# A conv-mixer block on one core: a norm's sum in four groups, sixteen native weight tiles, and a last pair of columns in halves

## The chip, the cores and the metric

The kernel runs on one core of a Trainium2 chip. The metric is the device time of one execution in microseconds (us), lower is better. Times of the instructions come from one profiled execution of the kernel.

## The reference

One decoder block in fp32 for 256 positions of width 2048. A condition vector c gives six modulation vectors of 2048 through a weight of 2048 by 12288. The mixer is a gated causal depthwise convolution; a squared-ReLU MLP of width 8192 follows.

```python
cond = silu(c)
sh1, sc1, g1, sh2, sc2, g2 = split(cond @ mod_w + mod_b, 6)
h = rms_norm(x, norm1_g) * (1.0 + sc1) + sh1
a, gt = split(h @ w_in + b_in, 2)            # 2048 -> 2 x 2048
u = a * sigmoid(gt)
u = depthwise_causal_conv(u, dw_w, 31 taps) + dw_b
y = silu(layer_norm(u, ln_g, ln_b)) @ w_out + b_out
x = x + (1.0 + g1) * y
h = rms_norm(x, norm2_g) * (1.0 + sc2) + sh2
x = x + (1.0 + g2) * (square(relu(h @ mlp_w1)) @ mlp_w2)
```

## The kernel before

Activations lie transposed: 128 features on the partitions, 256 positions along the free axis, so the width of 2048 is KT = 16 tiles called k. Weights are loaded as 1 MB tiles of 128 by 2048 in fp32.

**Two ways to multiply in fp32.** A *native* matmul takes the fp32 tiles as they are. A *split* one uses fp32r operands: ACT casts the weight to `hi`, DVE or POOL subtracts it to get `lo`, the activation is split in the same way into the two halves of `hl`, and PE adds hi times hi, hi times lo and lo times hi.

**The first stage.** `mod_c` holds rows of the modulation weight in a layout in which one output column group of 128 is a tile; `mod_col` forms one group on DVE as a multiply with the broadcast condition `cond` and an accumulated sum (line 299). For each k the scale column (SC1, finished as `amp`) and the shift column (SH1, finished as `modc`) are needed before h of that k exists. The load order is, for each k: scale column, shift column, and the tile `first` of k, which holds the rows of `w_in` for that k and all sixteen output tiles of the first eight jobs. These eight jobs are *held*: their sums stay in eight PSUM tiles (`mm`, `acc`, `small`, `row`) while k runs on the outside.

The loop over k issues on DVE, in a fixed order (`in_order`): the scale column of k, the low half of the activation of k - 1 (`act_low`, line 504), half of the weight's low part (`first_lo`, line 470) where k - 1 is split, for an even k the scaling of two x tiles by the norm factor r1 (line 514), the shift column, and the other half. ACT then forms h (line 523) and its high half (line 526), and PE multiplies. Ten of the sixteen k are in `NATIVE` and are multiplied natively (line 486); the other six are split (lines 463, 470 and 490 to 492).

**The first norm.** ACT squares x in eight pairs of tiles, PE adds over the partitions with a 128 by 128 matrix of ones (line 319), DVE scales the sum (line 336), ACT and DVE form the inverse root (lines 326 to 332) with one correction step. `rms_factor` is used again for the second norm.

**What follows.** ACT evacuates each held tile through a sigmoid and DVE multiplies (`gate`, lines 684 and 686). Jobs 8 to 15 are the remaining output pairs of `w_in`, each with two weight tiles (8,0), (8,1) and so on, split by ACT (line 200) and POOL (line 201), and multiplied in two halves of eight k each (lines 223 and 224). Between these matmuls lie steps of the modulation rows (line 241). Seven channel tiles are convolved on PE in a form that needs sixteen shifted copies of u on ACT each (`copy_wide`, line 646), one more with copies on both engines, the other eight on DVE tap by tap (lines 555 to 564). Then come layer norm, the output projection and the MLP, all with split weights.

**Order.** The order of instructions on each engine is settled when the program is built, by a scheduler that works with a simulated timeline, `issue_after` constraints and priorities (`urgent`). Loads are issued by SP in the order of one list; five `raw` buffers and four `first` buffers limit how far they run ahead. At run time each engine works its queue in order.

Of the kernel before, what the change touches and what calls it, by code (L numbers as in the profile page):

```python
# [14 lines left out]
P = 128  # L15
# [21 lines left out]
NATIVE = (1, 3, 5, 6, 8, 9, 11, 12, 14, 15)  # L37
# [20 lines left out]
SIDE = 14  # L58
POOLED = [("out", 0), ("out", 1), ("up", 0, 1), ("up", 0, 2)]
# [5 lines left out]
def conv_block(ctx: ExitStack, tc: tile.TileContext, x, vec, dwq, c_row, mod_r, mod_c, w_first, w_in, w_out, w1, w2, out):  # L65
# [48 lines left out]
    nc.scalar.activation(cz[:, :, 3], col("c", 0, KT), AF.Silu)  # L114
    modc = const.tile([P, 6 * KT], F32, name="modc")
# [3 lines left out]
    warm = const.tile([P, 1], F32, name="warm")  # L119

    def table(func, after):
        nc.scalar.activation(warm, after, func)
# [3 lines left out]

    raw = {}
# [3 lines left out]
    state = {"used": 0}  # L131
# [27 lines left out]
    def top_up():  # L159
        while todo and waiting[home(todo[0])] < room[home(todo[0])]:  # L160
# [13 lines left out]
            with tc.issue_after(state["load"].ins) if "load" in state else ExitStack():  # L174
                if key == ("first", KT - 1):
                    nc.sync.dma_start(raw[key][:, 0:HELD], source(key)[:, 0:HELD])
                    with tc.issue_after(state["load"].ins):
                        state["load"] = nc.sync.dma_start(raw[key][:, HELD:], source(key)[:, HELD:])
                else:
                    state["load"] = nc.sync.dma_start(raw[key], source(key))  # L180
# [7 lines left out]

    HALF = KT // 2
# [103 lines left out]

    def mod_col(at):
# [28 lines left out]
    def inverse_root(ms, src, scale, r, then=None):  # L323
# [114 lines left out]
    root_end = state["root_end"]  # L438
# [11 lines left out]
    first_parts = {}  # L450

    def first_hi(k):
        w = take(("first", k))
        if k in NATIVE:
            first_parts[k] = w
            return
        first_parts[k] = []
        for h in range(2):
# [489 lines left out]
```

## Time and profile before

| | us |
|---|---|
| Median of 3 runs | 1124.42 |
| Lowest and highest | 1123.18 and 1128.15 |
| The profiled execution's own time | 1122.33 |
| Its span, first to last instruction | 1120.5 |
| PE busy in the span | 1098.4 |
| DVE busy | 768.0 |
| ACT busy | 582.0 |
| POOL busy | 166.6 |

In a row of a timeline the first number is the start from the span's beginning, the second the duration, then engine, line, operation, output and inputs by the program's names, the shape, the count, and in brackets the idle time before it with what ended it. In a row of the windows the columns are the stretch, its length, the busy time of PE, of PE's weight loads, of DVE, ACT and POOL with instruction counts, the granted PE clock (1.00 is full), the mean share of the DMA engines and GB/s. A wait row gives the waiting instruction, what it waited for, the total, the count and the longest. A group row gives the instructions of one line with count, busy time, mean in ns, and the idle time before them.

### The profile page before, as it was taken

Reading aid. Unit: us, or ns where it says so; the run is one execution under the profiler, and the core shown is the slowest. Engines: PE = TensorE matmul, PEld = TensorE weight load, DVE = VectorE, ACT = ScalarE, POOL = GpSimd, SP = SyncE. Lnnn points to the kernel's source line nnn. Section 1 sums busy time; section 2 is a strip of 40 time slices with the busy share of each in tenths; the row PEclk is TensorE's granted clock in tenths of the full one; section 3 lists DMA queues with packets and bytes.
Section 4 is the critical chain, followed back from the end, with each engine's and each line's share of the span. In section 5 each row is a group of like instructions: output and inputs, shape, how many; then the busy total and the mean of one; then the engine's idle time right before and its main releaser. Section 6 shows DMA issues by size and latency. Waiting matters only on the chain.

```text
span 1120.5 us, 17425 instructions
## 1 busy us (share of the span) xinstructions
PE 1098.4 (98%) x7088; PEld 946.6 (84%) x7088; DVE 768.0 (69%) x1025; ACT 582.0 (52%) x806; POOL 166.6 (15%) x103
## 2 busy tenths in 40 slices
PE   6999999999999999999999999999999999999998
PEld 4888776766699998888888888888888888888888
DVE  3988689987489989887765555555555665555653
ACT  5222395664675587554445554444655444555441
POOL 0000086467533262000000000000000000000000
PEclk8999999999999999999999999999999999999999
DMA  9999979888599977888775555555554655555640
GB/s 384 420 421 420 418 307 346 349 322 318 207 390 350 371 283 276 290 350 299 273 259 192 190 193 194 193 191 193 189 190 165 211 188 188 188 188 188 209 139 29
DMA packets 41553, 293.35 MB, mean 262 GB/s; under 512 B 4609, under 2 KB 5121, under 8 KB 6401
## 3 DMA queue, kind: packets, MB, share of 16 engines
q1 hardware_dynamic: 41328, 292.17, 70.4%
q8 instruction: 55, 0.90, 0.3%
q14 instruction: 24, 0.20, 0.0%
q10 hardware_dynamic: 146, 0.08, 0.0%
HBM read 290.14 MB, written 2.10 MB: 261 GB/s over the span
## 4 chain that ended last, share of the span: by engine, by line
PE 86%; DMA 6%; DVE 6%; ACT 1%; issue 0%; POOL 0%; DVEq 0%; ACTq 0%; POOLq 0%
PE mm L223 45%; PE mm L224 24%; DMA raw<-mod_c 4%; PE mm L220 3%; DVE raw L299 3%; PE mm L219 3%; PE mm L221 3%; PE row L241 2%; PE mm L669 2%; DMA raw<-w_in 1%; PE small L319 1%; DVE lo L470 1%; PE mm L111 1%; PE mm L486 1%; PE acc L669 0%
## 5 line engine op out<-in xcount | busy, mean ns | idle before, releaser
L200 ACT ACTIVATE hi<-raw 128x1024 fp32r<-128x1024 f32 x320 | 335.3, 1057 | 355.9 <-PE mm L223 327.1
L201 DVE TENSOR_TENSOR lo<-raw,hi 128x1024 fp32r<-128x1024 f32 x272 | 333.6, 1232 | 234.4 <-ACT hi L200 233.4
L223 PE MATMUL mm<-hl,hi 128*128 128x512 f32 x1184 | 414.3, 393 | 0.4 <-DVE u L686 0.4
L223 PE MATMUL mm<-u,hi 128*128 128x512 f32 x1056 | 366.8, 390 | 0.0
L224 PE MATMUL mm<-hl,lo 128*128 128x256 f32 x1184 | 332.2, 281 | 0.0
L224 PE MATMUL mm<-u,lo 128*128 128x256 f32 x1056 | 297.7, 282 | 0.0
L223 PEld LDWEIGHTS mm<-hl,hi 128*128 128x128 f32 x1184 | 221.6, 187 | 58.2 <-issue 8.4
L223 PEld LDWEIGHTS mm<-u,hi 128*128 128x128 f32 x1056 | 198.2, 188 | 41.7 <-DVE small L332 0.2
L224 PEld LDWEIGHTS mm<-hl,lo 128*128 128x128 f32 x1184 | 223.7, 189 | 5.1 <-issue 4.2
L224 PEld LDWEIGHTS mm<-u,lo 128*128 128x128 f32 x1056 | 199.6, 189 | 0.1
L299 DVE SCALAR_TENSOR_TENSOR raw<-raw,cond 128x2048 f32<-128x2048 f32 x64 | 148.3, 2320 | 20.3 <-DMA raw<-mod_c 14.7
L201 POOL TENSOR_TENSOR lo<-raw,hi 128x1024 fp32r<-128x1024 f32 x48 | 118.1, 2482 | 198.0 <-ACT hi L200 198.0
L561 DVE SCALAR_TENSOR_TENSOR acc<-u,v,acc 128x256 f32<-128x256 f32 x224 | 94.7, 490 | 1.9
L220 PE MATMUL mm<-hl,hi 128*128 128x256 f32 x288 | 81.5, 284 | 0.8 <-DVE hl L209 0.8
L219 PE MATMUL mm<-hl,hi 128*128 128x256 f32 x288 | 80.5, 284 | 1.2 <-ACT hl L208 0.8
L221 PE MATMUL mm<-hl,lo 128*128 128x256 f32 x288 | 81.1, 283 | 0.0
L219 PEld LDWEIGHTS mm<-hl,hi 128*128 128x128 f32 x288 | 54.6, 192 | 2.8 <-ACT hl L208 1.7
L220 PEld LDWEIGHTS mm<-hl,hi 128*128 128x128 f32 x288 | 55.2, 192 | 1.6 <-DVE hl L209 1.2
L221 PEld LDWEIGHTS mm<-hl,lo 128*128 128x128 f32 x288 | 55.2, 192 | 0.0
L646 ACT ACTIVATE wide<-u 32x284 f32<-32x284 f32 x110 | 48.2, 438 | 2.7 <-DVE u L686 1.4
L423 ACT ACTIVATE two<-mm 128x512 f32<-128x512 f32 x70 | 40.9, 584 | 13.5 <-PE mm L224 13.5
L523 ACT ACTIVATE two<-two,modc,amp 128x256 f32<-128x256 f32 x16 | 9.6, 599 | 71.2 <-DVE modc L279 71.2
(166 smaller groups left out, 916.7 us busy)
## 6 DMA issues: line engine op xcount, KB each, us to landing
raw<-w SPq DMA_DIRECT2D x128, 1024.0 KB, 4.9
raw<-mod_c SPq DMA_DIRECT2D x64, 1024.0 KB, 10.8
raw<-mod_r SPq DMA_DIRECT2D x32, 1024.0 KB, 7.9
raw<-w_in SPq DMA_DIRECT2D x16, 1024.0 KB, 7.2
raw<-w_out SPq DMA_DIRECT2D x16, 1024.0 KB, 7.4
first<-w_first SPq DMA_DIRECT2D x15, 1024.0 KB, 16.1
x<-x SPq DMA_DIRECT2D x2, 1024.0 KB, 6.9
x<-x SPq DMA_DIRECT2D x1, 2048.0 KB, 9.8
```

The lines of the kernel that those rows point to most:

```text
L200: nc.scalar.activation(hi, w[:, ks, :], AF.Copy)
L201: end = engine.tensor_tensor(lo, w[:, ks, :], hi.bitcast(F32), op=ALU.subtract)
L219: nc.tensor.matmul(out_p, w, m[:, 0:T], start=begin, stop=False)
L220: nc.tensor.matmul(out_p, w, m[:, T : 2 * T], start=False, stop=False)
L221: state["mm_end"] = nc.tensor.matmul(out_p, lo[:, k % HALF, :], m[:, 0:T], start=False, stop=end)
L223: nc.tensor.matmul(p[:, c, :], hi[:, k % HALF, :], m, start=(k == 0), stop=(k == KT - 1))
L224: state["mm_end"] = nc.tensor.matmul(p[:, c, T : 2 * T], lo[:, k % HALF, :], m[:, 0:T], start=False, stop=(k == KT - 1), skip_group_check= ...
L241: state["row_end"] = nc.tensor.matmul(row_ps[0][32 * k : 32 * k + 32, :], cz[:, 4 * kg + k, 3 - b : 35 - b], w[:, 4 * k : 4 * k + 4, :], s ...
L299: nc.vector.scalar_tensor_tensor(w, w, 1.0, cb, op0=ALU.mult, op1=ALU.mult, accum_out=acc)
L423: nc.scalar.activation(t1, p[:, cs, T : 2 * T], AF.Copy)
L561: nc.vector.scalar_tensor_tensor(out, s, w, acc, op0=ALU.mult, op1=ALU.add)
L646: nc.scalar.activation(dst, src, AF.Copy)
```

## The change

Four things change. The first norm squares four pairs on ACT and four on DVE, and PE adds them with 32 columns of ones into four groups of 32 partitions, issued ahead of the first columns; one copy and one full matmul with the ones then add the groups up, each sum being there 32 times. The scaling of the sum is folded into the constants of the inverse root, in all three norms. All sixteen k are native, so the casts and subtractions of `first` tiles are gone. The two columns of the last k and its `first` tile are loaded in halves, and each of the two columns is formed by two half operations and one that adds the two sums. A table load for the inverse root is issued ahead.

```diff
-NATIVE = (1, 3, 5, 6, 8, 9, 11, 12, 14, 15)
+SPLIT_LOADS = [("col", SC1 * KT + KT - 1), ("col", SH1 * KT + KT - 1), ("first", KT - 1)]
...
+    table(AF.Abs_reciprocal_sqrt, cond[:, KT - 1, 0:1])
...
-                if key == ("first", KT - 1):
-                    nc.sync.dma_start(raw[key][:, 0:HELD], source(key)[:, 0:HELD])
-                    with tc.issue_after(state["load"].ins):
-                        state["load"] = nc.sync.dma_start(raw[key][:, HELD:], source(key)[:, HELD:])
+                if key in SPLIT_LOADS:
+                    first_half = nc.sync.dma_start(raw[key][:, 0:HALF], source(key)[:, 0:HALF])
+                    with tc.issue_after(first_half.ins):
+                        state["load"] = nc.sync.dma_start(raw[key][:, HALF:], source(key)[:, HALF:])
...
+    def mod_col_halves(at):
+        w = take(("col", at))
+        which, k = divmod(at, KT)
+        accs = [modc[:, at : at + 1], other]
+        for h in range(2):
+            ks = slice(h * HALF, (h + 1) * HALF)
+            in_order(lambda: nc.vector.scalar_tensor_tensor(
+                w[:, ks, :], w[:, ks, :], 1.0, cond[:, ks, :], op0=ALU.mult, op1=ALU.mult, accum_out=accs[h]
+            ))
+        in_order(lambda: nc.vector.scalar_tensor_tensor(
+            accs[0], accs[0], other, col("modb", at), op0=ALU.add, op1=ALU.add
+        ))
+        if which in amps:
+            in_order(lambda: nc.vector.tensor_tensor(amps[which][:, k : k + 1], accs[0], col("n1g", k), op=ALU.mult))
...
-        state["root_end"] = nc.scalar.activation(guess, guess, AF.Copy, scale=-0.5).ins
+        nc.scalar.activation(guess, guess, AF.Copy, scale=-0.5 * scale)
...
-        nc.vector.scalar_tensor_tensor(ms, ms, EPS, q, op0=ALU.add, op1=ALU.mult)
-        nc.vector.scalar_tensor_tensor(r, ms, 3.0, guess, op0=ALU.subtract, op1=ALU.mult)
+        nc.vector.scalar_tensor_tensor(ms, src, EPS / scale, q, op0=ALU.add, op1=ALU.mult)
+        nc.vector.scalar_tensor_tensor(r, ms, 3.0 / scale, guess, op0=ALU.subtract, op1=ALU.mult)
...
-    def rms_factor(total, ms, r):
-        nc.vector.tensor_scalar(ms, total, 1.0 / D, None, op0=ALU.mult)
-        return inverse_root(ms, total, 1.0 / D, r)
+    def rms_factor(total, ms, r, times=1):
+        return inverse_root(ms, total, 1.0 / (times * D), r)
...
-    mods(by_col(0))
     p = ps.tile([P, 512], F32, name="small", bufs=1)
     for k2 in range(HALF):
         s = two()
-        nc.scalar.activation(s, pair_of(xs, k2), AF.Square)
-        column_sum(p[:, 0:T], [s[:, j, :] for j in range(2)], k2 == 0, k2 == HALF - 1)
-    r1 = tmp.tile([P, T], F32, name="r", bufs=1)
-    rms_factor(p[:, 0:T], p[:, T : 2 * T], r1)
+        if k2 < HALF // 2:
+            nc.scalar.activation(s, pair_of(xs, k2), AF.Square)
+        else:
+            nc.vector.tensor_tensor(s, pair_of(xs, k2), pair_of(xs, k2), op=ALU.mult)
+        for j in range(2):
+            g = (2 * k2 + j) % 4
+            nc.tensor.matmul(p[32 * g : 32 * g + 32, 0:T], ones[:, 0:32], s[:, j, :], start=k2 < 2, stop=k2 >= HALF - 2)
+    mods(by_col(0))
+    with urgent():
+        part = two()[:, 0, :]
+        nc.scalar.activation(part, p[:, 0:T], AF.Copy)
+        p = ps.tile([P, 512], F32, name="row", bufs=1)
+        nc.tensor.matmul(p[:, 0:T], ones, part, start=True, stop=True)
+        r1 = tmp.tile([P, T], F32, name="r", bufs=1)
+        rms_factor(p[:, 0:T], p[:, T : 2 * T], r1, 32)
...
     def first_mm(k, h):
+        w = take(("first", k))
         with tc.issue_after(state["step_end"].ins) if k else ExitStack():
...
+                    step = nc.tensor.matmul(
+                        held[n][:, c, :], w[:, 2 * n + c, :], h, start=k == 0 and c == 0, stop=k == KT - 1, skip_group_check=True
+                    )
...
-            first_lo(k - 1, 0)
...
-            first_lo(k - 1, 1)
-            if k - 1 not in NATIVE:
-                first_mm(k - 1, None)
...
-        first_hi(k)
-        if k in NATIVE:
-            first_mm(k, h)
+        first_mm(k, h)
```

With the change the scheduler also writes other orders for the work behind the held tiles. ACT's queue from the first held tile on, in the kernel before and in the changed one (tiles in w_in's jobs named by job and half):

```
before:  gate 0; hi of 8,0 (2); gates 1, 2; hi of 8,1 (2); gates 3 to 7; wide x10; hi of 9,0 (2);
         wide x7; hi of 9,1 (1); wide x2; hi of 9,1 (1); wide x12; evacuation of job 8; ...
changed: gates 0 to 4; hi of 8,0 (2); gates 5 to 7; wide x11; hi of 8,1 (2); wide x7; hi of 9,0 (2);
         wide x3; hi of 9,1 (2); wide x11; evacuation of job 8; ...
```

On POOL the nine memsets' place moves from behind the third low half of job 8 to behind the first: they wait for the end of the held tiles. From job 10 on up to the output projection the order on ACT and POOL is nearly the same; around the first jobs of the MLP a few casts and modulations change places on ACT and DVE.

More of the change, by code (lines that the diff above doesn't have):

```diff
@@ L114, in conv_block @@
     nc.scalar.activation(cz[:, :, 3], col("c", 0, KT), AF.Silu)
+    state = {"used": 0}
     modc = const.tile([P, 6 * KT], F32, name="modc")
@@ L118, in conv_block @@
     amps = {w: const.tile([P, KT], F32, name=f"amp{w}") for w in (SC1, SC2)}
-    warm = const.tile([P, 1], F32, name="warm")
+    warm = const.tile([P, 2], F32, name="warm")
+    other = warm[:, 1:2]
     def table(func, after):
-        nc.scalar.activation(warm, after, func)
+        nc.scalar.activation(warm[:, 0:1], after, func)
+    table(AF.Abs_reciprocal_sqrt, cond[:, KT - 1, 0:1])
     def urgent():
         return tc.high_priority(offset=URGENT)
+    HALF = KT // 2
     raw = {}
@@ L448, in conv_block @@
     held += [pair(ps.tile([P, 512], F32, name=name, bufs=1)) for name in ("small", "row")]
-    first_parts = {}
-    def first_hi(k):
-        w = take(("first", k))
-        if k in NATIVE:
[L455 to L458, printed above, removed]
-            js = slice(h * HELD, (h + 1) * HELD)
-            hi = wts.tile([P, HALF, P], F32R, name="hi", bufs=6)
-            lo = wts.tile([P, HALF, P], F32R, name="lo", bufs=6)
-            with tc.issue_after(root_end):
-                nc.scalar.activation(hi, w[:, js, :], AF.Copy)
-            first_parts[k].append((hi, lo, w[:, js, :]))
-    def first_lo(k, h):
-        if k in NATIVE:
-            return
-        hi, lo, w = first_parts[k][h]
-        in_order(lambda: nc.vector.tensor_tensor(lo, w, hi.bitcast(F32), op=ALU.subtract))
     def in_order(op):
```

23 lines of the change are left out of this document (4 added, 19 removed).

## The prediction

> **What bounds the kernel now.** I read the page first, then the windows table by stage, then the waits of PE, then the timelines of each engine around the end of the first projection (k = 0 to 15 into eight held tiles).
>
> ```profile
> PE 1098.4 (98%) x7088; PEld 946.6 (84%) x7088; DVE 768.0 (69%) x1025; ACT 582.0 (52%) x806; POOL 166.6 (15%) x103
> 20.00:30.00 10.00, 4.39 (x25) 4.39 (x26) 7.51 (x9) 5.39 (x8) 0.00 (x0) 0.66 1.02 423
> 40.00:60.00 20.00, 19.25 (x131) 17.95 (x130) 19.82 (x24) 5.06 (x8) 0.00 (x0) 1.00 1.01 420
> 120.00:140.00 20.00, 18.34 (x103) 16.38 (x102) 11.80 (x17) 6.21 (x11) 2.68 (x2) 1.00 1.02 417
> PE mm L490 <- ACT hl L526: 6.1, 1, 6.1
> PE acc L492 <- DVE lo L470: 5.1, 6, 1.5
> PE mm L219 <- ACT hl L208: 0.8, 1, 0.8
> ...
> PE mm L223 <- DVE u L686: 0.4, 1, 0.4
> ```
>
> PE is 98% busy, yet up to 140 us the last three columns (clock, DMA share, GB/s) show the DMA engines full at 417 to 423 GB/s: there the stream sets the pace. The first two wait rows are PE's idle time in that stage. The last two are the first and last of the five waits that remain after 141 us, 2.8 us together. So from 141 us the end is PE's work, and the change is worth what it does to the time at which PE leaves the first projection, less any new wait behind it.
>
> **The first projection.** Where does the stream leave it?
>
> ```profile
> 94.24 2.29 DVE L299 SCALAR_TENSOR_TENSOR raw<-raw,cond 128x2048 f32<-128x2048 f32 x1 [1.56 <-DMA raw<-mod_c]
> 109.18 2.29 DVE L299 SCALAR_TENSOR_TENSOR raw<-raw,cond 128x2048 f32<-128x2048 f32 x1 [1.57 <-DMA raw<-mod_c]
> 116.75 2.29 DVE L299 SCALAR_TENSOR_TENSOR raw<-raw,cond 128x2048 f32<-128x2048 f32 x1 [2.27 <-DMA raw<-mod_c]
> 119.09 0.22 DVE L301 SCALAR_TENSOR_TENSOR amp<-modc,v 128x1 f32<-128x1 f32 x1
> 119.22 0.42 DVE L504 TENSOR_TENSOR hl<-two,hl 128x256 fp32r<-128x256 f32 x1
> 119.56 1.22 DVE L470 TENSOR_TENSOR lo<-first,hi 128x1024 fp32r<-128x1024 f32 x1
> 120.69 0.69 DVE L514 TENSOR_TENSOR two<-x,r 128x512 f32<-128x512 f32 x1
> 121.29 2.29 DVE L299 SCALAR_TENSOR_TENSOR raw<-raw,cond 128x2048 f32<-128x2048 f32 x1
> 123.62 0.16 DVE L279 TENSOR_TENSOR modc<-modc,v 128x1 f32<-128x1 f32 x1
> 123.88 0.60 ACT L523 ACTIVATE two<-two,modc,amp 128x256 f32<-128x256 f32 x1 [6.57 <-DVE modc L279]
> 126.99 3.62 PE L486 MATMUL mm<-two,first 128*128 128x256 f32 x16
> 133.90 3.62 PE L486 MATMUL mm<-two,first 128*128 128x256 f32 x16
> 139.94 1.03 PE L486 MATMUL row<-two,first 128*128 128x256 f32 x4
> L463 ACT ACTIVATE hi<-first 128x1024 fp32r<-128x1024 f32 x12 | 12.0, 1045 | 7.9 <-DMA first<-w_first 7.9
> L470 DVE TENSOR_TENSOR lo<-first,hi 128x1024 fp32r<-128x1024 f32 x12 | 14.6, 1219 | 0.0
> 25.61 0.80 PE L490 MATMUL mm<-hl,hi 128*128 128x256 f32 x2 [6.10 <-ACT hl L526]
> 29.14 0.28 PE L491 MATMUL mm<-hl,hi 128*128 128x256 f32 x1
> ```
>
> The three DVE rows that waited for a column tile are scale tiles of k = 11, 13 and 14: two k take 14.94 us, so the stream gives a k every 7.47 us. A native k costs PE 133.90 - 126.99 = 6.91 us. Sixteen native k fit inside the stream; twelve casts on ACT (12.0 us) and twelve subtractions on DVE (14.6 us) go. The bytes stay, so the tile of k = 14 still lands at 116.75.
>
> After it the changed kernel's DVE does, by the distances between these starts: scale column 2.34, amp 0.13, hl 0.34, no L470, scaling 0.60, shift column 2.33. Its modc starts at 122.5 instead of 123.62. ACT's step starts 0.26 later and takes 0.60: h of k = 14 is there at 123.4. PE is free then: by the same count without the scaling, from 109.18, k = 13 starts at 115.2 and lasts to 122.1. So k = 14 runs 123.4 to 130.3 and k = 15 130.3 to **137.2**, against 139.94 + 1.03 = 140.97 now: **3.8 us earlier**.
>
> *The halves of k = 15* are covered. Its scale tile lands near 116.75 + 7.47 = 124.2; whole, as now, the same count (no scaling in an odd k) gives h at 130.2, just ahead of PE at 130.3. A half operation has no row; it lies between half of 2.29 and all of it. At half, the last one starts when the last half tile lands, near 126.7, and h comes at 128.9, while PE is still on k = 14: worth 0. At the other end, four full ones from 123.0 on, h would come at 133.7, 3.4 on the path. It is half the elements of the same instruction, and I take half. The extra DMA issues on SP are 1 MB tiles cut in two, queued behind a full stream: 0.
>
> *The first norm.* Sixteen matmuls of 32 columns in four groups replace sixteen of 128 columns, half the squares move to DVE, a fold and a copy come, a scaling on DVE goes. PE starts at 25.61 now. Were that unchanged, fourteen native k and about 1.6 us of slow start (25.61 to 29.14 runs at about half pace) would put k = 14 at 123.9, 0.5 later than the stream allows. Any gain of 0.5 us there hides it; more is worth nothing. I take 0, with 0.5 as the bound. The second norm loses the same scaling; its factor is used two jobs later, and PE shows no wait for it: 0.
>
> **The second stage, where a wait appears.** Job 8 is the first job after the held tiles. Its weights are cast by ACT and subtracted by POOL before PE can go.
>
> ```profile
> 119.17 8.31 SPq L180 DMA_DIRECT2D raw<-w_in  x4
> raw<-w_in SPq DMA_DIRECT2D x4, 1024.0 KB, 14.2
> 135.82 0.47 ACT L684 ACTIVATE two<-mm,v 128x256 f32<-128x256 f32 x1 [4.62 <-PE mm L486]
> 136.19 1.99 ACT L200 ACTIVATE hi<-raw 128x1024 fp32r<-128x1024 f32 x2
> 138.80 2.01 ACT L200 ACTIVATE hi<-raw 128x1024 fp32r<-128x1024 f32 x2
> 142.12 0.51 ACT L684 ACTIVATE two<-row,v 128x256 f32<-128x256 f32 x1
> 142.48 4.49 ACT L646 ACTIVATE wide<-u 32x284 f32<-32x284 f32 x10
> 137.32 7.06 POOL L201 TENSOR_TENSOR lo<-raw,hi 128x1024 fp32r<-128x1024 f32 x3 [135.39 <-ACT hi L200]
> 140.62 0.58 PE L223 MATMUL mm<-hl,hi 128*128 128x512 f32 x1
> 151.79 0.99 PE row L241 x8
> 149.02 3.15 ACT L646 ACTIVATE wide<-u 32x284 f32<-32x284 f32 x7
> ```
>
> Now: both weight tiles are cast by 140.8, between the first gates, and POOL's three first halves end at 144.38. PE passes from the held tiles to job 8 without a wait; 30.5 of its 32 steps take 140.97 to 151.6, so 0.35 each and 11.2 for the job: it would end at 152.2 without the row step at 151.79.
>
> The changed kernel's ACT queue has another order: five gates, the two casts of weight 8,0, three gates, **eleven wide copies**, and only then the casts of weight 8,1. Call PE's end of the held tiles E. The first weight has landed (119.17 + 14.2 = 133.4).
>
> - Gate 4 waits for held tile 4, which is done 2.6 before E; it ends at E - 2.1, and the casts run to E - 0.1, the first half ready at E - 1.1. POOL at 2.35 a half (7.06 / 3) is done with it at E + 1.3. PE has begun with its hi steps, waits, and ends the first half at E + 3.9.
> - POOL's short memsets (0.35) come between; the second half is ready at E + 4.1, and PE ends weight 8,0 at E + 6.7.
> - Gates 5 to 7 wait for E itself (gate 5 reuses a buffer that the last k reads): E + 1.3. Eleven copies at 0.45 take to E + 6.3, the first cast of 8,1 to E + 7.3, POOL to E + 9.7. PE waits from E + 7.0 for it; two quarters of 2.7 end the job at **E + 15.1**, 3.9 later than 11.2 would.
>
> With E = 137.2 that is 152.3, against 152.2 now. Next, the first half of weight 9,0: seven more copies (3.15) and its cast reach E + 12.5, POOL E + 14.9; PE, with a row step of 0.99 first, asks at E + 16.3. From there PE is the bound again.
>
> **Sum.** 1122.33 (the profiled execution; its span is 1120.5) - 3.8 + 3.9 + 0 for the rest = 1122.4. The median of the runs shown, 1124.42, lies 2.1 above the profiled one, so I forecast **1124.5**.
>
> **A rule weighed.** The waits of the new stage are at E + 0.2 to 1.3 and E + 7.0 to 9.7, 2.7 us the longer. The rows: waits of up to 1.5 us left the clock at 1.00 (120 to 140), one of 6.1 us left 0.66 in its ten (20 to 30), which is at most 10 x 0.34 = 3.4 us of PE time. 2.7 lies between, nearer to 1.5; I take no drop and keep 3.4 as the end.
> [...]
>
> **The rivals.**
> - *The gain survives.* If ACT reaches the casts of 8,1 as early as now (copies late or cheap, so that ACT's order doesn't bind), PE goes on unbroken and 3.8 us remain: 1120.7; with half the wait, 1122.6. For: only 1.5 us of ACT work beside the copies has to move. Against: each engine's queue runs in order, and the eleven copies stand before those casts.
> - *PE leaves a little earlier.* If the scaling of k = 14 fell into the wait before, as DVE's order does not have it, E would be 136.6. The same 15.1 follow: 1123.9.
> - *Slower.* The wait before weight 8,1 reaches the length at which the clock falls: one drop adds up to 3.4, 1127.9; a drop at the first wait too, 1131.3. [...] For: the window 20 to 30. [...]
> - *The native steps bind.* If a native k took PE over 7.47, E would slip by 16 times the excess. The 6.91 between the two native k above speak against it.
>
> **How the numbers follow.** Forecast 0.62 (with the second rival inside it, 1123 to 1126), gain survives 0.20, slower 0.13, native steps or a late wait in the reordered later stages 0.05. A difference of 0.5%, 5.6 us, is about what a measurement of this kernel can tell from no change. The most that can be won is 3.8 + 0.6 and the 2.8 us of later waits; passing 5.6 needs nearly all of it: 0.02. Losing 5.6 needs two clock drops or a wait of that size further on: 0.04. The rest, 0.94, lies within. Range: down to the surviving gain, 1120.7, up to one full clock drop or the 3.4 of four full half columns, 1127.9.
>
> **What would show it.** The k = 14 scale column starts at 116.7 and PE's last held matmul ends near 137.2; if it is 141, the first stage is wrong. Among PE's waits stand two new ones of about 1.1 and 2.7 for POOL's lo, within 11 us of that end; if they are missing and the span is near 1117, the second stage is wrong. The granted clock from 137 to 160 is 1.00. DVE's half columns take 1.2 each. Waits after 155 stay near 3 us in all.

## The result and the profile after

The changed kernel takes **1130.57 us** (median of 22 runs, 1127.70 to 1135.05) against 1125.09 for the kernel before on the same chip: ratio **1.0042, interval 1.0029 to 1.0055**. The interval lies wholly above 1: a small loss, at 0.42% under the 0.5% that the prediction called about what a measurement can tell from no change. The time is 6 us over the forecast and over the range's upper end, 1127.9. The profiled execution took 1128.72 us with a span of 1126.9 (before 1122.33 and 1120.5), so the traces differ by 6.4 us.

The page's row of busy times, rows of the windows, and some of the waits of PE over the whole span of the changed kernel:

```profile
PE 1103.9 (98%) x6994; PEld 946.2 (84%) x6994; DVE 757.0 (67%) x1020; ACT 569.6 (51%) x792; POOL 166.0 (15%) x103
120.00:140.00 20.00, 17.50 (x81) 14.76 (x80) 14.36 (x29) 8.18 (x17) 2.89 (x10) 1.00 1.02 414
140.00:160.00 20.00, 18.06 (x98) 13.40 (x100) 16.15 (x42) 19.52 (x37) 16.70 (x8) 0.91 0.70 242
300.00:320.00 20.00, 18.38 (x138) 14.46 (x137) 12.52 (x19) 16.17 (x30) 12.59 (x10) 0.91 0.99 399
PE mm L483 <- ACT two L514: 7.4, 5, 4.1
PE mm L222 <- DVE hl L211: 2.0, 2, 1.7
PE mm L226 <- POOL lo L203: 1.9, 1, 1.9
PE mm L226 <- POOL u L102: 1.7, 1, 1.7
PE mm L221 <- ACT hl L210: 1.4, 1, 1.4
PE mm L225 <- DVE two L440: 0.9, 3, 0.3
```

ACT and DVE do less than before (569.6 and 757.0 us), yet PE is busy for 5.5 us more. In two stretches the clock is 0.91 where it was 1.00, and a slower matmul counts as a longer busy one (0.63 us in place of 0.41 for a 512-wide one from 148 to 152 us): that is 3.4 of the 5.5 us, as the next paragraphs show. The first wait row belongs to the first projection; the others lie behind it.

**The first projection** came as forecast (timeline of DVE, then PE):

```profile
116.91 2.29 DVE L316 SCALAR_TENSOR_TENSOR raw<-raw,cond 128x2048 f32<-128x2048 f32 x1 [2.16 <-DMA raw<-mod_c]
122.65 0.16 DVE L281 TENSOR_TENSOR modc<-modc,v 128x1 f32<-128x1 f32 x1
126.38 1.22 DVE L302 SCALAR_TENSOR_TENSOR raw<-raw,cond 128x1024 f32<-128x1024 f32 x1
123.56 3.72 PE L483 MATMUL mm<-two,first 128*128 128x256 f32 x16 [0.84 <-ACT two L514]
130.57 3.62 PE L483 MATMUL mm<-two,first 128*128 128x256 f32 x16
136.61 1.03 PE L483 MATMUL row<-two,first 128*128 128x256 f32 x4
```

PE leaves the held tiles at 136.61 + 1.03 = 137.64 (forecast 137.2, before 140.97). A half column takes 1.22, and the last one, which starts at 127.53, is done before PE begins k = 15 at 130.57.

**Behind it** (ACT, POOL and PE of the changed kernel):

```profile
135.97 2.00 ACT L202 ACTIVATE hi<-raw 128x1024 fp32r<-128x1024 f32 x2
138.94 4.93 ACT L635 ACTIVATE wide<-u 32x284 f32<-32x284 f32 x11
143.89 2.01 ACT L202 ACTIVATE hi<-raw 128x1024 fp32r<-128x1024 f32 x2
137.11 2.36 POOL L203 TENSOR_TENSOR lo<-raw,hi 128x1024 fp32r<-128x1024 f32 x1 [135.18 <-DMA raw<-w_in]
145.03 4.71 POOL L203 TENSOR_TENSOR lo<-raw,hi 128x1024 fp32r<-128x1024 f32 x2 [2.83 <-ACT hi L202]
139.53 0.38 PE L226 MATMUL mm<-hl,lo 128*128 128x256 f32 x1 [1.66 <-POOL u L102]
147.44 0.39 PE L226 MATMUL mm<-hl,lo 128*128 128x256 f32 x1 [1.94 <-POOL lo L203]
148.01 0.41 PE L225 MATMUL mm<-hl,hi 128*128 128x512 f32 x1
148.43 0.63 PE L225 MATMUL mm<-hl,hi 128*128 128x512 f32 x1
150.99 0.63 PE L225 MATMUL mm<-hl,hi 128*128 128x512 f32 x1
```

The eleven wide copies stand before the casts of 8,1, as forecast, and PE waits twice, 1.66 and 1.94 us. (The row of the first wait names a memset on POOL; the low half that PE needs ends just before it, at 137.11 + 2.36 = 139.47.) Behind the second wait the 512-wide matmul takes 0.63 in place of 0.41 until about 151.6: the clock, which is 0.50 for 3.41 us from 148.27 on and so costs 1.7. The first convolution matmul starts at 170.61, before at 168.21: instead of 3.3 early it is 2.4 late.

**Around the layer norm** the rest goes. Two rows of the kernel before, then those of the changed kernel:

```profile
314.49 6.91 POOL L201 TENSOR_TENSOR lo<-raw,hi 128x1024 fp32r<-128x1024 f32 x2 [4.33 <-ACT hi L200]
317.80 1.35 DVE L201 TENSOR_TENSOR lo<-raw,hi 128x1024 fp32r<-128x1024 f32 x1 [1.39 <-ACT hi L200]
```

```profile
306.93 0.50 PE L221 MATMUL mm<-hl,hi 128*128 128x256 f32 x2 [1.40 <-ACT hl L210]
317.58 4.77 POOL L203 TENSOR_TENSOR lo<-raw,hi 128x1024 fp32r<-128x1024 f32 x2 [5.81 <-ACT hi L202]
316.45 1.06 ACT L202 ACTIVATE hi<-raw 128x1024 fp32r<-128x1024 f32 x1 [1.73 <-PE mm L222]
320.90 2.54 DVE L203 TENSOR_TENSOR lo<-raw,hi 128x1024 fp32r<-128x1024 f32 x1 [2.18 <-ACT hi L202]
323.36 1.27 DVE L211 TENSOR_TENSOR hl<-acc,hl 128x512 fp32r<-128x512 f32 x2
324.10 0.39 PE L222 MATMUL mm<-hl,hi 128*128 128x256 f32 x1 [1.74 <-DVE hl L211]
```

The output projection begins here; its activations come in eight pairs of tiles from the layer norm. PE waits 1.40 for the first pair (before it stood 0.39 for a row tile and 0.80 for the pair) and the clock falls, again to 0.50 for 3.41 us, from 308.69. A cast on ACT waits 1.73 for PE, and the rest of ACT's queue with it; the slower PE can be a reason, but two kernels below, x3_whole and x9_native_fill, have the late last pair without a clock drop ahead of it (0.99 and 0.98 from 300 to 320 us, with the drop behind the wait). The `lo` subtraction on DVE takes 2.54 in place of 1.35: it starts while POOL's second one of the same kind runs and ends 1.1 after it. In the kernel before it starts just before POOL's first one ends, and there it is POOL's two that are long, 6.91 in place of 4.77. The last pair's `hl` stands behind it on DVE, and PE waits 1.74 for that (0.55 before). In the ten traces that have this subtraction in front of the last pair the wait is its duration less 0.8: 1.35 and 0.55 in the kernel before, 2.54 and 1.74 here, 3.31 and 2.51 in x9_native_fill, 3.44 and 2.64 in x3_whole.

A table of where the time is lost, in us against the trace of before: the first row is the first convolution matmul, the others the starts of single evacuation copies (ACT, 128x512 from `mm`). The kernels beside after are explained below.

| place (time before) | after | x1_native | x4_order | z3_native_pool_cols |
|---|---|---|---|---|
| convolution starts (168.21) | +2.4 | -2.3 | -1.2 | -2.1 |
| last in jobs (269.48) | +1.6 | -3.5 | -2.3 | -3.3 |
| first quarter of the MLP (451.90) | +5.1 | -0.3 | +1.2 | +0.8 |
| from 530 to the end (1105.61) | +6.3 | +4.2 | +2.4 | +0.8 |

The traced execution of before took 1122.33 us, near the fast end of that kernel's executions, whose medians beside the experiments were 1123.6 to 1126.3 (1124.0 over the 57 of them with a granted clock of 0.997, 1128.7 over the 27 with 0.994 or less), so a kernel at +2.4 here can have the same median.

From the last in job to the first quarter of the MLP the changed kernel loses 3.5 us against before, and the trace accounts for them: PE idles 4.2 us in that stretch where it idled 2.5, and the clock takes 1.7. In x1_native it is the same: 3.2 lost, 3.9 us of idling, and a clock drop of 1.7.

### The profile page after: what moved, and what is told of

Same layout as the page of the kernel before. It is cut to its first block, busy times and chain, and to the rows that moved or that the text cites. A ratio compares the mean times of both kernels' runs of the same rounds, so it can differ in the third digit from the quotient of the medians.

```text
span 1126.9 us, 17218 instructions
## 1 busy us (share of the span) xinstructions
PE 1103.9 (98%) x6994; PEld 946.2 (84%) x6994; DVE 757.0 (67%) x1020; ACT 569.6 (51%) x792; POOL 166.0 (15%) x103
## 4 chain that ended last, share of the span: by engine, by line
PE 77%; DMA 13%; DVE 5%; issue 3%; ACT 2%; POOL 0%; DVEq 0%; SPq 0%; ACTq 0%; POOLq 0%
PE mm L225 39%; PE mm L226 21%; DMA raw<-mod_c 12%; PE mm L222 3%; PE mm L221 3%; PE mm L223 3%; DVE raw L316 3%; PE row L243 2%; PE mm L658 2%; DVE lo L203 1%; DMA x<-x 1%; PE mm L483 1%; ACT hi L202 1%; POOL lo L203 0%; ACT wide L635 0%
## 5 line engine op out<-in xcount | busy, mean ns | idle before, releaser
L316 DVE SCALAR_TENSOR_TENSOR raw<-raw,cond 128x2048 f32<-128x2048 f32 x62 | 144.5, 2334 | 44.8 <-DMA raw<-mod_c 44.7
L483 PE MATMUL mm<-two,first 128*128 128x256 f32 x256 | 61.4, 395 | 7.4 <-ACT two L514 7.4
L483 PEld LDWEIGHTS mm<-two,first 128*128 128x128 f32 x256 | 50.3, 198 | 17.1 <-ACT two L514 10.0
```

What stands on the lines that cost most here:

```text
L316: nc.vector.scalar_tensor_tensor(w, w, 1.0, cb, op0=ALU.mult, op1=ALU.mult, accum_out=acc)
L483: step = nc.tensor.matmul(held[n][:, c, :], w[:, 2 * n + c, :], h, start=k == 0 and c == 0, stop=k == KT - 1, skip_group_check=True)
```

## The experiments

Ratios are to the kernel before on the same chip. Theory A: the lead of 3.3 us is real; the order on ACT returns it, with a clock drop on top; behind the norm there is a second loss. Rivals: the new norm or the halves cost by themselves, or native tiles as such slow PE.

### What in the first two stages costs: x1, x2, x3, x4, x7

**x1_native**: the kernel before with one line changed.

```diff
-NATIVE = (1, 3, 5, 6, 8, 9, 11, 12, 14, 15)
+NATIVE = tuple(range(KT))
```

> The kernel before with one part of the change: all sixteen k native; norm, scaling and whole columns as before. In its ACT queue the casts of weight 8,1 stand behind one wide copy, not eleven. Theory A (the order of ACT's queue behind the held tiles costs the time): PE leaves the held tiles near 137.7 us, waits about 0.3 us for POOL's first half and not at all before weight 8,1, the clock stays at 1.00 from 137 to 160, and the time is 3 us below before, a ratio of 0.997. Theory B (the native steps or what they do to the first projection cost it): the time is above before as in the changed kernel, a ratio of 1.004, and the end of the held tiles or the waits behind it show it.

Measured: 1126.31 us, 0.9995 (0.9974 to 1.0016). The first two stages came as theory A has it: PE leaves the held tiles at 138.38, waits 0.28 for job 8, the clock stays at 1.00, and the convolution starts 2.3 early. The ratio of 0.997 didn't come. The lead is lost around the norm and in the MLP, where a column product waits 2.37 for its tile ahead of the evacuation's sum:

```profile
497.55 2.29 DVE L299 SCALAR_TENSOR_TENSOR raw<-raw,cond 128x2048 f32<-128x2048 f32 x1 [2.37 <-DMA raw<-mod_c]
502.12 0.68 DVE L424 TENSOR_TENSOR two<-mm,two 128x512 f32<-128x512 f32 x1
502.85 0.79 PE L223 MATMUL mm<-u,hi 128*128 128x512 f32 x1 [2.91 <-DVE two L424]
```

**x2_norm**: the kernel before with the new first norm alone. The lines show its sum; the folded constants of all three norms and the early table load belong to it.

```diff
...
+        for j in range(2):
+            g = (2 * k2 + j) % 4
+            nc.tensor.matmul(p[32 * g : 32 * g + 32, 0:T], ones[:, 0:32], s[:, j, :], start=k2 < 2, stop=k2 >= HALF - 2)
...
```

> The kernel before with the new first norm alone (four groups, no scaling step); held tiles and columns as before. Theory: the norm has nothing to do with the loss, as the prediction had it: the last held matmul ends within 0.5 us of 140.97, the time is 1124 to 1126.5 us. Rival: its sum and table load shift the order of the first columns, the last held matmul ends over 1 us later or earlier, and the whole time moves by over 2 us.

Measured: 1125.29 us, 1.0013 (0.9996 to 1.0030). The last held matmul ends at 141.22 (140.97 before), and the end comes 0.7 later: the norm by itself changes nothing that can be told from noise, as forecast.

**x3_whole**: the changed kernel with whole columns.

```diff
-SPLIT_LOADS = [("col", SC1 * KT + KT - 1), ("col", SH1 * KT + KT - 1), ("first", KT - 1)]
+SPLIT_LOADS = [("first", KT - 1)]
```

> The changed kernel with the two columns of the last k whole again. The scheduler then puts the casts of weight 8,1 behind one wide copy. Theory A: the halves themselves are worth nothing, but their presence moved the casts; without them the held tiles end within 0.5 us of the changed kernel's 137.6, the wait before weight 8,1 is gone, the ratio to before is 0.997. Theory B (norm or native steps cost the time): 1.004 as in the changed kernel. If the halves are worth something by themselves, the held tiles end over 0.5 us later than 137.6.

Measured: 1126.35 us, 1.0002 (0.9981 to 1.0024). The ratio of 0.997 didn't come here either. PE leaves at 138.14, so the halves are worth 0.5 us there. But the order on ACT is another one: one wide copy before the casts of 8,1 in place of eleven, a wait of 0.29, clock 1.00 from 140 to 160, and the convolution at 165.69. The half columns thus cost 4.9 us at that place (170.61), most of it through the order that the scheduler writes when they are there (x4_order, next), and not by their own work.

**x4_order**: the changed kernel with that order alone undone.

```diff
...
         if n in COPY_AT:
-            copy_wide(COPY_AT[n], False)
+            with tc.issue_after(cast_end) if n == HELD else ExitStack():
+                copy_wide(COPY_AT[n], False)
```

> The changed kernel with one constraint more: the wide copies of job 8 come after the casts of weight 8,1. All edits stay. Theory A: the wait of 1.7 us at the end of the held tiles stays, the one of 1.9 before weight 8,1 goes and the clock drop of 1.8 us behind it; conv starts 1 to 2 us earlier than before instead of 2.4 later; if the later losses (3.5 us around the layer norm, 1.1 in the MLP) hang on the clock or the phase that came with it, the ratio is 0.998. Theory C (the later losses come from later orders and have nothing to do with the casts): conv starts 1 to 2 us earlier, but the 4.6 us come again: 1.002 to 1.003.

Measured: 1126.96 us, 1.0014 (0.9996 to 1.0031); the convolution starts at 167.06. Of the two waits one is left, and it leaves the clock alone (PE, and the window):

```profile
139.54 0.39 PE L226 MATMUL mm<-hl,lo 128*128 128x256 f32 x1 [1.67 <-POOL u L102]
140.00:160.00 20.00, 19.91 (x117) 14.56 (x116) 16.18 (x43) 19.49 (x39) 18.19 (x8) 1.00 0.73 268
```

One constraint gives back 3.6 us at the convolution and about two thirds of the difference in time. This is theory C: what is lost later comes again (4.7 us, from -2.3 to +2.4 in the table), and the expected 1.002 to 1.003 lies within the interval.

**x7_both**: x4_order, and the casts of the out weights behind the norm's last activation pair.

```diff
...
-            splits(jobs[n + 1])
+            with tc.issue_after(state["hi_end"]) if n == KT else ExitStack():
+                splits(jobs[n + 1])
```

> As x4_order, and the casts of weight 1,1 of the output projection wait in ACT's queue until the last activation pair behind the layer norm is done. Theory: three casts of 1.05 us leave the path of pairs 6 and 7, which ACT feeds at 1.7 us a pair to a PE that needs 1.43; the wait of PE for a late pair (1.7 us in the changed kernel, 0.6 in the kernel before) goes. 1 us less than x4_order, a ratio of 0.997, and a smaller scatter. Rival: the weight 1,1 then comes late itself and PE waits for it, no gain or 1 to 2 us more than x4_order.

Measured: 1125.78 us, 1.0007 (0.9991 to 1.0022). The wait for the last pair is 0.2 in place of 1.7, but a wait of 2.5 for DVE's sum into x (`x<-mm,x`) stands behind it; at the end it is where x4_order is (+2.3 and +2.4). Delaying the casts moves the wait.

### The order and the clock by themselves: xd, x6

**xd_late**: the kernel before with the bad order forced on it.

```diff
-    with tc.issue_after(state["sg"].ins):
-        split_w(jobs[HELD] + (1,), nc.gpsimd)
...
+        if n == HELD:
+            copy_wide(COPY_AT[n], False, 11)
+            with urgent(), tc.issue_after(state["wide"]):
+                split_w(jobs[HELD] + (1,), nc.gpsimd)
```

> The kernel before with one thing changed: the casts of weight 8,1 stand behind eleven wide copies in ACT's queue, as the changed kernel has them. Theory A (that order is what cost the gain): PE waits some 4.2 us before weight 8,1 (the third half of POOL comes near 151.0, PE asks at 146.8) and the clock falls after it; the first conv matmul starts 4 to 6 us later than before, the ratio is 1.004 to 1.006. Theory B (the order is harmless by itself, the native steps or the norm cost the time): below 1.002.

Measured: 1128.83 us, 1.0023 (1.0004 to 1.0042). PE waits 0.91 and 1.00 for casts at 148 and 150 us, the clock there stays 1.00, and the evacuation at 160.56 comes 2.2 late. The order costs the kernel before some 2 us by the waits alone. Neither theory is met: PE waits less than the 4.2 us of theory A and no clock falls there, but the ratio is above the 1.002 of theory B.

**x6_fill**: the changed kernel with four spare matmuls in the 1.9 us in which PE stood.

```diff
...
+                if n == HELD and c == 0:
+                    for _ in range(FILL):
+                        state["fill_end"] = nc.tensor.matmul(
+                            p[:, 1, :], parts[job + (0,)][1][0][:, 0, :], hl[0][:, 0, :], start=True, stop=True
+                        )
```

> The kernel after, with four spare matmuls of the weight of tile 8,0 put on PE between the matmuls of 8,0 and 8,1, where PE stood 1.9 us for the cast of 8,1; their result is overwritten. Theory (the clock fell because PE stood): the granted clock of 140 to 160 us is 1.00 in place of 0.91, the first convolution matmul comes at 168.5 to 169.0 in place of 170.61, and the time is 1127 to 1129.5 us, less what the norm takes again. Rival (the drop has another cause, the denser matmuls of the native tiles): the clock stays near 0.91 and the convolution starts no earlier than 170.6.

Measured: PE row and window:

```profile
147.28 0.39 PE L227 MATMUL mm<-hl,lo 128*128 128x256 f32 x1 [1.11 <-POOL lo L204]
140.00:160.00 20.00, 18.89 (x110) 13.48 (x109) 15.96 (x41) 19.49 (x37) 16.72 (x8) 1.00 0.71 270
```

The wait ends at the same time (147.28 and 147.44), but the clock is 1.00 and the convolution starts at 168.89, 1.7 earlier. So some 1.6 us of the 5.7 that the changed kernel loses from the end of the held tiles to this point (32.97 us against 27.24) are the clock, and 3.6 the two waits; 0.5 stay open. The first wait is still there, 1.67: that the clock would have fallen behind the second one without it was not tried. The time of the whole did not follow: 1131.78 us, 1.0058 (1.0038 to 1.0077), over the 1127 to 1129.5 expected, since more is lost behind the norm (clock 0.91 and 0.83 from 300 to 340).

### Behind the norm: xb, x9, xa, y1, y2

**xb_fill** (kernel before, two spare matmuls ahead of the norm's first pair), **x9_native_fill** (x1_native with three) and **xa_all** (x9 with x7's edit, and two modulation columns moved from up jobs of the MLP's first quarter to its down jobs). The lines show the spare matmuls:

```diff
...
+        if job == ("out", 0):
+            with tc.issue_after(state["row_end"].ins):
+                for _ in range(FILL):
+                    nc.tensor.matmul(p[:, 1, 0:T], ones, v[:, 0:T], start=True, stop=True)
```

> The kernel before with two spare native matmuls on PE behind the modulation rows, where PE waits for the first activation pair behind the layer norm (0.86 us of work in a wait of 0.8); their result is overwritten. Theory (part of the executions of the kernel before lose clock after that wait, and from it the 3 to 5 us that its slower executions show): the scatter narrows, the median comes to 1123 to 1124, a ratio of 0.998 to 0.999. Rival (the scatter comes from elsewhere): 1.000, the scatter as before.

> x1_native with three such spare matmuls (1.29 us in a wait of 1.4). Theory: the granted clock stays at 1.00 from 300 to 320 and the wait of 1.7 us for the late pair goes with it, since that pair's cast waits for a slowed PE; the 3.2 us that x1_native lost between job 14 and the MLP shrink below 1. The MLP's wait of 2.9 us near 500 may stay. A ratio of 0.996 to 0.998. Rival (the loss there comes from ACT's queue, whatever the clock): x1_native's 0.9995 again.

> x9_native_fill with the casts of weight 1,1 of the output projection behind the last activation pair, and two of the late modulation columns moved from the first up jobs to the first down jobs. Theory: neither the wait of 1.7 us behind the layer norm nor that of 2.9 us near 500 is left, and the 3 us won at the held tiles come through: the ratio is 0.996 to 0.997, 1121 to 1122. Rival: DMA, which is full from 300 to 330, or the buffers of its tiles bind the MLP's first quarter, PE waits at another place, and the ratio stays above 0.999.

Measured: 1123.73 us, 0.9992 (0.9974 to 1.0009); 1125.01 us, 0.9991 (0.9975 to 1.0007); 1124.90 us, 0.9996 (0.9982 to 1.0011). The wait for the first pair is gone in all three and the clock from 300 to 320 is 1.00, 0.98 and 1.00. xb_fill can't be told from the kernel before. x9_native_fill misses its 0.996 to 0.998 and xa_all its 0.996 to 0.997: x9 loses 5 us between the last in job (-3.4) and 451.90 (+1.6), with a wait of 2.5 for the last pair behind a `lo` subtraction of 3.31 on DVE; xa has 4.4 for x instead. The clock at the first pair was not the whole of it, and the clock falls behind each of these waits too (0.93 and 0.83 from 320 to 340).

**y1_lo** (x9) and **y2_mended** (x4_order with the spare matmuls): DVE's `lo` subtractions of the out weights behind the last `hl`.

```diff
...
+            behind = engine is nc.vector and key[0] == "out"
+            with tc.issue_after(state["hl_end"]) if behind else ExitStack():
...
```

> The kernel before with all held tiles native, three spare matmuls on PE ahead of the first pair after the norm, and VectorE's lo subtractions of the out weights put behind the last hl subtraction of the norm. Theory (PE waits for the last pair because a lo subtraction slowed from 1.35 to 3.31 us by GpSimd's stands ahead of it): the wait of 2.5 us falls to 0.6 or less, the evacuation at 451.90 of the kernel before comes 0.5 to 2 us early in place of 1.6 late, and the time is 1121 to 1123.5 us. Rival (the weights of out 2 then come late by as much, or the MLP's columns take it): the same wait stands 10 to 30 us later, and the time is 1124 to 1126.5 us.

> The kernel after, mended in three places: the wide copies of job 8 behind the casts of 8,1, the three spare matmuls ahead of the first pair after the norm, and VectorE's lo subtractions of the out weights behind the last hl subtraction. Theory: all of what the change lost is found in these three places; the lead of 2.3 us over the kernel before at the last in job is held beyond the norm, the time is 1121.5 to 1124 us. Rival: something behind the norm takes the lead whatever stands in its way, and the time is 1124.5 to 1127 us.

Measured: 1133.47 us, 1.0079 (1.0060 to 1.0099), and 1135.67 us, 1.0095 (1.0074 to 1.0115). The wait for the last pair is 0.2, but my constraint let the scheduler put the four subtractions of out 2, the third job of the output projection, behind other work (DVE, then PE, of y1_lo):

```profile
329.73 4.63 DVE L204 TENSOR_TENSOR lo<-raw,hi 128x1024 fp32r<-128x1024 f32 x4
331.00 0.39 PE L226 MATMUL mm<-hl,lo 128*128 128x256 f32 x1 [3.68 <-DVE lo L204]
```

Both rivals were right in kind, and the price was larger than I gave. They show that the wait for the last pair goes with the subtraction in front of it; of what that wait costs the whole they tell nothing.

### The subtractions on another engine: z0 to z5

**z0_pool** (kernel before), **z1_pool** (x9), **z2_mended_pool** (x4_order with the spare matmuls): the `lo` subtractions of out 2 on POOL.

```diff
-POOLED = [("out", 0), ("out", 1), ("up", 0, 1), ("up", 0, 2)]
+POOLED = [("out", 0), ("out", 1), ("out", 2), ("up", 0, 1), ("up", 0, 2)]
```

> The kernel before with the lo subtractions of out 2 on GpSimd and nothing else. Theory (there the subtraction took 1.35 us and PE waited 0.55 us for the last pair): the time moves by under 1 us, 1123 to 1125.5 us. Rival (GpSimd is too slow for these weights, 2.4 us each): a wait for the weights of out 2 near 330 to 350 us and 1126 to 1131 us.

> The kernel before with all held tiles native, three spare matmuls on PE ahead of the first pair after the norm, and the lo subtractions of out 2 on GpSimd in place of VectorE. Theory (the lead is lost to a lo subtraction in front of the last pair): the wait of 2.5 us near 318.8 us is 0.6 or less, the evacuation that the kernel before has at 451.90 comes 1 to 3 us early, and the time is 1120.5 to 1123.5 us. Rival (the stage is limited by the casts and subtractions as a whole, wherever they stand): a wait of 1.5 us or more for the weights of out 2 stands between 325 and 350 us, and the time is 1124 to 1130 us.

> The kernel after with the wide copies of job 8 behind the casts of 8,1, the three spare matmuls, and the lo subtractions of out 2 on GpSimd. Theory: the lead of 2.3 us at the last in job is held beyond the norm, no wait over 0.6 us for the last pair, 1121 to 1124 us. Rival: a wait for the weights of out 2 in its place, 1124 to 1130 us.

Measured: z0 1128.36 us, 1.0028 (1.0008 to 1.0047); z1 1123.81 us, **0.9976 (0.9957 to 0.9994)**; z2 1126.52 us, 1.0020 (1.0000 to 1.0039). With the subtraction gone from DVE the wait for the last pair falls from 2.5 (x9) to at most 0.2 in z1 and z2: that wait's cause is shown. But the evacuation at 451.90 is at +0.6 in z1, not 1 to 3 early as the theory had it: a wait of 2.2 for a cast of a later weight and 0.8 for its `lo` follow near 387 us, and the clock falls behind them (0.96 from 360 to 400, 1.7 us). z1's median lies just above its expected 1120.5 to 1123.5; its interval overlaps that of x9 (0.9975 to 1.0007), so that the move gains time over x9 is not shown. z2 missed: its 1126.52 is in the rival's range. In the kernel before the same move has no lead to protect, and z0 is slower; its trace, which took 1134.79, has the wait near 390 us and one of 3.8 for the evacuation sum near 500 us.

**z5_pool_cols** (z1 and the two moved columns), **z4_half_cols** (the same with only one of the two out 2 weights on POOL), **z3_native_pool_cols** (z5 without spare matmuls). The lines show the columns:

```diff
-LATE_UP = [0, 0, 1, 1, 1, 1, 2, 2]
+LATE_UP = [0, 0, 1, 1, 1, 1, 1, 1]
-LATE_DOWN = [1] * 8
+LATE_DOWN = [2, 2, 1, 1, 1, 1, 1, 1]
```

> z1_pool with two MLP columns one job earlier or later. Theory: the wait of 1.1 us near 500 to 530 us goes, the wait of 2.2 us for a cast stays, and the time is 0.5 to 2 us under z1_pool's 1123.8 us, 1121.8 to 1123.3. Rival: the columns then hold up something else, 1123.5 to 1126 us.

> All held tiles native, three spare matmuls, only the first of the two weights of out 2 on GpSimd, and two MLP columns one job earlier or later so that no column product stands before an evacuation. Theory: without the slowed pair of lo subtractions on VectorE the later wait for a cast goes too; waits behind the norm under 1.5 us in all, the lead at the end 1 to 3 us, time 1120 to 1123 us. Rival (the stage of the out weights takes the lead in any order): another wait of 2 us or more between 320 and 400 us, 1123.5 to 1127 us.

> z5_pool_cols without the three spare matmuls. Theory (the spare matmuls cover a wait of 1.4 us that costs clock besides): the wait is there, the clock between 300 and 340 us is 0.91 in 20 us, and the time is 1.5 to 3 us above z5_pool_cols. Rival: the matmuls only fill a wait that costs nothing more, and the two times agree within 1 us.

Measured: z5 1123.60 us, 0.9977 (0.9962 to 0.9993); z4 1126.78 us, 1.0004 (0.9993 to 1.0016); z3 **1123.31 us, 0.9973 (0.9959 to 0.9988)**. The waits of PE in z3, two from 280 to 325 us and two from 345 to 400:

```profile
PE mm L219 <- ACT hl L208: 1.4, 1, 1.4
PE mm L220 <- DVE hl L209: 0.2, 1, 0.2
PE mm L219 <- ACT hi L200: 2.2, 1, 2.2
PE mm L221 <- DVE lo L201: 0.8, 1, 0.8
```

No wait is left from 400 to 530, so the columns' part did what it was for. z3 and z5 agree within 0.3 us: the spare matmuls are worth nothing, and in z3's trace the wait of 1.4 left the clock at 1.00. z4, expected at 1120 to 1123, has a new wait of 2.3 for x. By its median z3 is 3 us of 1126 faster than the kernel before, and the changed kernel was 0.4% slower than that: native tiles, out 2 on POOL, two columns moved, and neither the new norm nor the halves. Where these 3 us come from the traces don't show. z3's own trace, at its median, ends 0.8 later than the trace of before, which lies under that kernel's median; and the intervals of z3 and x1_native (0.9974 to 1.0016) overlap.

## Why the prediction was wrong, step by step

- *PE leaves the first projection 3.8 earlier:* 3.3. The stream at 7.47 a k, the count of DVE's steps (modc at 122.65, said 122.5) and native steps inside the stream were right.
- *The halves are worth 0:* their own work gained 0.5 at that point. What I did not see is that the order on ACT, which I priced, was their doing (x3_whole). It changes nothing in the sum.
- *The first norm 0:* right (x2_norm 1.0013, interval across 1).
- *Two waits, giving back 3.9:* right in place, cause and order. Their lengths were 1.66 (said 1.1) and 1.94 (said 2.7); 3.6 in all, as the first came later than said and left less for the second.
- *"I take no drop":* **the first step that failed.** The clock fell behind the wait of 1.94, to 0.50 for 3.41 us (148.27 to 151.68), and the drop cost 1.6 to 1.7 us (x6_fill), not the 3.4 that I kept as its end. I compared lengths of waits, and in the rival too the drop was to come at a longer wait; it came at one shorter than the 2.7. No run shows a length at which the clock falls: here the waits of 1.94 and 1.40 have a drop behind them, those of 1.66 and 1.74 have none (the last section).
- *"From there PE is the bound again", and "0 for the rest":* **the step that failed by most.** From the last in job (+1.6) to the end (+6.3) another 4.7 were lost: 3.5 around the norm and the out projection, 1.2 in the MLP's first quarter, there in three waits of 0.3 and 0.5 that stay open. Of the 3.5, a second clock drop is 1.7 and longer waits are the other 1.7. The two drops together are 3.4 of the 6.3 us by which the trace misses the sum. I read waits of 2.8 us after 141 as a stage that only follows. My reading now, argued and not shown, is that ACT, DVE, POOL and PE have less slack there than the 2 to 3.5 us by which the change moves the arrival. x1_native, x3_whole and x4_order came to the norm 2.3 to 3.5 early and left the first quarter of the MLP at -0.3, +2.5 and +1.2.
- *The rivals:* "the gain survives" held for the second stage once the order was mended (x4_order, x1_native), not for the program. "Slower" named the clock drop that came and, for one drop, 1127.9; 1130.57 needed the norm's loss too. Its 1131.3 for two drops is near by luck: two came, but the second at the norm, and at half the price. The chance of 0.05 for "a late wait in the reordered later stages" and the 0.04 for losing 5.6 us are where the result fell.

What stays open: why the norm's stage loses about the same when it is reached early as when it is reached late. The sums agree (a first pair 1.4 late, a last pair 1.7 late, one clock drop), but what makes these waits come at either arrival was not found. The waits that were taken away one by one (first pair, last pair, x, columns) were mostly followed by another. With native tiles and out 2 on POOL (z1, z3, z5) the median came under that of before, but none of these traces has a lead left at 451.90. Whether the `hi` buffers, ACT's queue or DVE sets the last wait of 2.2 near 387 us was not tried.

## What to carry to other kernels

Price a gain in one stage only as far as the next stage with little slack on its helper engines, and look there for waits of a few tenths: such a stage turned an early arrival into other waits as readily as a late one here. Price a wait of PE with what the clock may add to it: here 1.7 us on top of a wait of 1.4 to 2.2, in some traces and not in others. Where a scheduler writes the order, test each part of a change with the order that it gets: here the part that did the least work, the halves, moved eleven copies in front of a cast and cost 3.6 us at the convolution. One constraint in the right place (x4_order) took back most of what the change had lost; the lowest ratio, z3_native_pool_cols, keeps one part of the change and moves work off the engine whose queue held up a wait, though what gave its time is not shown.

## What the hardware showed that I had not expected

- The clock did not go by the length of a wait. It was lower in the 20 us around a wait of 1.94 (0.91) and of 1.40 (0.91, also in x1_native), and stayed at 1.00 with waits of 1.67 (x4_order) and 1.4 (x2_norm, z3_native_pool_cols). In the changed kernel's trace each of the two slow stretches is 3.41 us at 0.50, and their starts, 148.27 and 308.69, lie 160.42 us apart, 47.0 times 3.413. Counted in steps of 3.413 us from these starts, the four steps from 20 us on with the most time without a matmul are those from 144.86 and 305.28, with 1.94 and 1.62 us and a slow step behind them, and those from 322.35 and 138.03, with 1.74 and 1.50 us and full clock behind them. In the kernel before the slow stretch is 6.83 us at 0.50 from 21.97, within the wait of 6.10 that ends at 25.61 and behind it; counted from there no later step has more than 1.41, and the clock is 1.00 from 28.80 to 1121.06. Rows of the changed kernel, then two stretches of z2_mended_pool and two of z3_native_pool_cols (PE's busy time is the second figure behind the stretch, the clock the third from the end):

```profile
138.03:141.44 3.41, 1.91 (x11) 1.70 (x12) 3.37 (x9) 3.35 (x9) 3.41 (x10) 1.00 0.95 396
144.86:148.27 3.41, 1.47 (x8) 0.93 (x7) 3.41 (x10) 3.33 (x8) 3.24 (x2) 1.00 0.48 199
148.27:151.68 3.41, 3.41 (x13) 2.93 (x11) 3.41 (x10) 3.34 (x6) 2.94 (x2) 0.50 0.31 55
305.28:308.69 3.41, 1.79 (x14) 1.33 (x11) 2.71 (x5) 3.28 (x7) 3.41 (x4) 1.00 1.09 459
322.35:325.76 3.41, 1.67 (x15) 1.66 (x14) 3.41 (x4) 1.15 (x3) 0.01 (x1) 1.00 0.87 308
325.76:329.17 3.41, 3.41 (x32) 3.41 (x31) 1.41 (x4) 1.24 (x2) 0.00 (x0) 1.00 0.78 233
385.42:388.83 3.41, 1.61 (x14) 1.41 (x12) 3.38 (x5) 1.73 (x3) 0.00 (x0) 1.00 0.94 324
388.83:392.24 3.41, 2.28 (x17) 2.07 (x18) 2.44 (x3) 3.39 (x6) 1.40 (x2) 1.00 1.01 418
384.72:388.13 3.41, 0.80 (x5) 0.39 (x3) 3.09 (x4) 3.04 (x5) 0.00 (x0) 1.00 0.97 380
388.13:391.54 3.41, 3.09 (x14) 3.10 (x15) 1.40 (x2) 3.38 (x6) 2.10 (x2) 0.50 0.96 363
```

z2_mended_pool and z3_native_pool_cols have the same two waits there, 2.17 and 0.76. In z2's rows 1.80 us of idling lie in the first stretch and 1.13 in the second, and the clock is 1.00 in both; in z3's 2.61 lie in the first, and in the second the clock is 0.50.

So the same waits cost 1.7 us more in z3 (3.41 at 0.50) and nothing more in z2's rows. What decides between them is not shown: no run moved a wait by itself, and a stretch with 1.62 us of idling had a drop behind it where those with 1.74 and 1.80 had none.
- A 128x1024 subtraction on DVE took 1.22 to 1.23 us with POOL idle (324.72 to 332.28 in the kernel before). Where it began while POOL ran one of the same kind, it ended 1.07 to 1.09 us after that one (1.09 in the kernel before, 1.08 here, 1.07 in x1_native, 1.09 in x9_native_fill), and so took 1.35, 2.54, 2.54 and 3.31. POOL's took 2.40 and 2.41 here; in the kernel before, where a column product and then this subtraction ran on DVE beside them, 3.58 and 3.38.
